# A hybrid encoder layer: rotary rows of q and k gathered into one tile by transfers, turned together and taken back

## The chip, the cores and the metric

The kernel runs on one core of one Trainium2 chip, in one launch. The metric is the device time of an execution in microseconds (us). The kernel before takes 788.81 us (median of three runs, 788.7 to 789.13).

## What is computed

One layer for 512 tokens of width 1024, all in float32. Cut to what matters here:

```python
def rope_partial(t, pos):            # ROT_DIM = 16 of HEAD_DIM = 64, half = 8
    t1, t2, tp = t[..., :half], t[..., half:ROT_DIM], t[..., ROT_DIM:]
    return jnp.concatenate([t1 * cos - t2 * sin, t1 * sin + t2 * cos, tp], axis=-1)

proj = h @ w_in[l]                   # 16 heads of q and 4 of k, v (A); 12 heads of q, k, v (B)
qa, ka, va, qb, kb, vb = jnp.split(proj, SPLITS, axis=-1)
qa, ka, qb, kb = (rope_partial(x, pos) for each, by heads)
o_a = windowed_gqa_sink(qa, ka, va, a_sink[l])       # mixer A: |i - j| <= 128, a sink per head
o_b = dilated_mixture(qb, kb, vb)                    # mixer B: three dilated windows, merged
g_a, g_b = jnp.split(jax.nn.sigmoid(h @ w_gate[l] + b_gate[l]), N_BRANCH, axis=-1)
y = (g_a * (o_a @ w_br_a[l]) + g_b * (o_b @ w_br_b[l])) @ w_out[l]
h = layer_norm(DN_ALPHA * h + y, ln1_g[l], ln1_b[l])
f = (jax.nn.silu(h @ w_ff_gate[l]) * (h @ w_ff_up[l])) @ w_ff_down[l]
h = layer_norm(DN_ALPHA * h + f, ln2_g[l], ln2_b[l])
```

Only the first 16 of each head's 64 features turn; the other 48 pass through.

## The kernel before, in words

**Numbers.** Every float32 operand of a product is split into a high part (rounded to float32r) and a low part (the rest), and a product is three products of parts: high by high, high by low, low by high. Weights arrive as float32 tiles of 128 x 512 (`load`, L335), a copy makes the high part (`copy`, L327 on ACT or L329 on VectorE) and a VectorE subtraction the low one (`split`, L348; in the dense layer `parts` and `tt`, L1091).

**Stages.** The input x, features on partitions, is split into `xh`, `xl` (L424). A unit of 1024 weight columns gives 128 output features by 512 tokens, 24 products of 512 columns (`feat_k`, L448 to L450). Units of q, k, v and the gates run in the order of the string `ORDER`: `q1` is a unit of q for mixer A (two heads), `k1` a unit of its k, `VA` its values, `A0` to `A3` the four head groups of mixer A, `Q01`, `K01` and so on q and k of mixer B, `V0` to `V2` its values, `B0` to `B3` its four heads, `G` a gate unit whose result is stored to DRAM until needed, `g` one that stays. The first units of k, q and v run before the string. Then come the branch products, the output product with the first norm (tokens on partitions, L979 to L981), the dense layer in a Strassen-like form (L1197 to L1199, L1326 to L1328), and the second norm, from which the result is stored.

**q and k.** `dense_q` and `dense_k` put a unit's sum into a PSUM bank. `rotate` (L466) turns all 128 rows, two heads: a product with a cosine table (L468), a shuffle of partitions (L470), a product with a sine table (L472) and a sum (L474). The tables are 128 x 512, with ones and zeros in the rows that don't turn. `q_post` and `k_post` then make the high and low parts of each head (L498, L516).

**Mixer A.** `unit_a` does one group of four heads for 128 tokens: scores (L532, L533), softmax (L654, L658, L614), turns of the probabilities by TensorE (L626), products with the values (L671, L672), and at the end one VectorE sum for each of the four heads (L683) into eight tiles `oaT`. The values of mixer A are turned by TensorE at L565. At most two such units, of A and B together, are under way (`UNITS = 2`).

**The order of the work.** No loop of the source is the order on the engines. `Program` collects every operation with its reads, writes, a priority (the planned PE time at which it is wanted, less a look-ahead: `LOOK` = 130 us for weight loads) and a cost for each engine that may do it. `run` plays these in planned time, gives each engine the most urgent operation that is ready and whose buffers fit, and issues the instructions in that order, so every engine's order is fixed when the program is built. Buffers are counted: 85 tiles of 128 x 512, of them six for arriving weights (`ws`), twelve for split weights (`whl`), 16 for attention, ten for the mixers' results and 41 for the rest (`gen`) as long as attention runs. After the last unit of attention, `free_all` gives the general class 64 and the split weights up to 40 within the whole. In the plan a transfer of SP takes 0.45 us of queue, then 0.65 us and its own cost, and lands 0.9 us later; copies from PSUM (`cp_alts`) may go to ACT or VectorE.

Of the kernel before, what the change touches and what calls it, by code (L numbers as in the profile page):

```python
# [15 lines left out]
P = 128  # L16
S = 512
# [44 lines left out]
N_WS, N_WHL, N_ATT, N_WHL1 = 6, 12, 16, 40  # L62
# [9 lines left out]
VA q1 A0 G q2 q3 G A1 G k1 q4 G q5 A2 G q6 G q7 A3 G2  # L72
Q00 K00 Q01 K01 Q02 K02 V0 V1 V2 B0 B1 g2 Q10 K10 Q11 K11 Q12 K12 B2 B3 g6
# [212 lines left out]
def hybrid_layer(ctx: ExitStack, tc: tile.TileContext, wpack, xT, xtok, sink, bgate,  # L286
# [7 lines left out]
    N_SLOT = 85  # L294
    pr = Program({"slot": N_SLOT, "bank": 8, **BANKS,
                  "ws": N_WS, "whl": N_WHL, "att": N_ATT, "gen": N_SLOT - 10 - N_ATT - N_WS - N_WHL,
                  "unit": UNITS, "st": 4, "x4": 4, "wf": N_WF})
# [53 lines left out]
    LOOK, LOOK_W, LOOK_U, LOOK_T = 130.0, 30.0, 15.0, (-300.0, -118.0, -114.5, -108.0)  # L351

    def half_unit(u, j):
        st, h, l = slot(F32, "ws"), slot(F32R, "whl"), slot(F32R, "whl")
        load(st, wpack[u, :, j * S:(j + 1) * S], prio=-LOOK)
        split(st, h, l, prio=-LOOK, hold=[(l, "room")])
        return h, l
# [29 lines left out]
    def unit(u):  # L387
        return [half_unit(u, 0), half_unit(u, 1)]
# [38 lines left out]
    load(cosT, ropec, abs_prio=-119.5)  # L427
    load(sinT, ropes, abs_prio=-119.4)
# [35 lines left out]
    SHUF = list(range(8, 16)) + list(range(0, 8)) + list(range(16, 32))  # L464

    def rotate(ps):  # L466
        R, Sh = slot(), slot()
        op([(DVE, dve(S))], lambda e: nc.vector.tensor_tensor(R.t, ps.t, cosT.t, op=ALU.mult),  # L468
           reads=[ps, cosT], writes=[R], prio=EV)
        op([(DVE, dve(S, extra=0.03))], lambda e: nc.vector.stream_shuffle(Sh.t, ps.t, SHUF), reads=[ps], writes=[Sh],  # L470
           prio=EV)
        op([(DVE, dve(S))], lambda e: nc.vector.tensor_tensor(Sh.t, Sh.t, sinT.t, op=ALU.mult),  # L472
           reads=[Sh, sinT], writes=[Sh], prio=EV)
        op([(DVE, dve(S))], lambda e: nc.vector.tensor_tensor(R.t, R.t, Sh.t, op=ALU.add),  # L474
           reads=[R, Sh], writes=[R], prio=EV)
        return R

# [8 lines left out]
    def q_post(ps, nt, kv_half):  # L486

        R = rotate(ps)
        out_ = []
        for hh in range(2):  # L490
# [3 lines left out]
            t = slot(F32R)  # L494
            op(cp64(), lambda e, t=t, a=a, hr=hr: copy(
                e, view(t.t[hr:hr + 64], nt, False), view(R.t[a:a + 64], nt, True)),
               reads=[R], writes=[(t, "h"), (t, "room")], prio=EV)
# [3 lines left out]
               reads=[R, (t, "h")], writes=[(t, "l")], prio=EV)  # L501
            out_.append((t, hr))
        return out_

    def k_post(ps, nt):

        R = rotate(ps)
        out_ = []
        for hh in range(2):
            a, c = 64 * hh, 64 - 64 * hh  # L510
            t, kl = slot(F32R), slot(F32R)
            for d, key in ((a, "h"), (c, "d")):
# [122 lines left out]
    oaT = [slot(F32, "res") for _ in range(8)]  # L635
    obT = [slot(F32, "res") for _ in range(2)]

    def unit_a(g, b, qs, kk, vs):
# [47 lines left out]
        lasts.append(op([(DVE, 1.19)], add, reads=[o, t, (U, 0)], writes=[(oaT[2 * g], b), (oaT[2 * g + 1], b)]))  # L686
# [160 lines left out]
    def dense_q(u, nt, kv_half):  # L847
        ps = bank("dense")
        feat_x(ps, unit(u))
        return q_post(ps, nt, kv_half)  # L850

    def dense_k(u, nt):
        ps = bank("dense")
        feat_x(ps, unit(u))
        return k_post(ps, nt)
# [5 lines left out]
    ka = k_post(psk, 4)  # L861
    qa = q_post(psq, 4, (0, 0))
    load(mB, maskb, prio=0)
    env = {"gate": 0, "qs": {}, "ks": {}}

    def step(w):
        if w == "VA":
            env["va"] = turned_values(U_VA, 4, 0, psv)
        elif w[0] == "q":
            i = int(w[1])  # L870
            kv = (i // 2) % 2
            qa.extend(dense_q(U_QA + i, 4, (kv, kv)))
        elif w == "k1":
            ka.extend(dense_k(U_KA + 1, 4))
# [8 lines left out]
        elif w[0] in "QK":  # L883
            pair, g = int(w[1]), int(w[2])
            u = U_QKB + 6 * pair + 2 * g + (w[0] == "K")
            if w[0] == "Q":
                env["qs"][pair, g] = dense_q(u, 4 if g == 0 else 0, (0, 1))
            else:
                env["ks"][pair, g] = dense_k(u, 8 if g == 0 else 0)
# [19 lines left out]
    def split_of(src, toks, prio=0.0):  # L909
        h, l = slot(F32R), slot(F32R)  # L910
        op(cp_alts(S), lambda e: copy(e, h.t, src.t), reads=toks, writes=[h, (l, "room")], prio=prio)
        op([(DVE, dve(S))], lambda e: nc.vector.tensor_tensor(l.t, src.t, f32(h.t), op=ALU.subtract),
# [13 lines left out]
    sa = [split_of(t, [(t, b) for b in range(NR)], -20) for t in oaT]  # L926
# [41 lines left out]
    def tok_major(nk, last, us_of, u0, g, b, finish, fine, alpha=ALPHA):  # L968
# [23 lines left out]
        res = [(k, us_of(k), unit(u0 + k)) for k in range(nk - last, nk)]  # L992
# [113 lines left out]
    TP = {}  # L1106
# [378 lines left out]
```

## Time and profile before

| | us |
|---|---|
| median of 3 runs | 788.81 |
| the profiled execution, its own time | 789.7 |
| its span, first to last instruction | 787.9 |
| PE busy | 776.5 |
| VectorE (DVE) busy | 668.6 |
| ScalarE (ACT) busy | 463.6 |
| GpSimd (POOL) busy | 116.9 |

The granted TensorE clock is 0.998 of 2.4 GHz over the span. PE is TensorE's products, PEld its weight loads, SP the queue that issues most transfers. A row of the trace gives a line of the kernel, an engine, an operation, the tiles it writes and reads (`sl` is any of the 128 x 512 tiles, `ps` a PSUM bank) and what ended the engine's idle time before it. Products overlap, so the length of one is longer than the distance from its start to the next one's.

### The profile page before, as it was taken

What the parts mean: (1) busy time and instruction counts of PE and PEld (TensorE: products, weight loads), DVE (VectorE), ACT (ScalarE), POOL (GpSimd) and SP (SyncE); (2) the same over time, 40 slices, a digit from 0 to 9 for tenths busy, and PEclk for the clock granted to TensorE, in tenths of its full rate; (3) what the DMA queues carried; (4) which work ended last, traced back from release to release, by engine and by line L of the source; (5) the groups of instructions that cost most, each with busy time, mean ns of one, the idle gap of its engine ahead of it and who ended that gap; (6) DMA issues with size and microseconds to landing.
All of it is one profiled execution on the core that took longest, in us unless ns stands there. A gap on an engine that the chain in (4) does not pass through costs nothing.

```text
span 787.9 us, 13456 instructions
## 1 busy us (share of the span) xinstructions
PE 776.5 (99%) x4634; PEld 688.3 (87%) x4634; DVE 668.6 (85%) x1413; ACT 463.6 (59%) x1013; POOL 116.9 (15%) x284
## 2 busy tenths in 40 slices
PE   8999999999999999999999999999999999999995
PEld 5788888888998888888888899999999999999984
DVE  5898999899766999678596999888888889888888
ACT  5655675766755675787251567655655566555710
POOL 0000101000024000610020011133112330123000
PEclk9999999999999999999999999999999999999999
DMA  7533122412131122427563188779876977689102
GB/s 258 210 94 117 58 94 69 141 61 81 44 105 55 51 79 86 173 87 271 169 156 81 41 218 228 185 175 196 225 196 154 233 190 210 179 214 211 53 1 106
DMA packets 61124, 109.42 MB, mean 139 GB/s; under 512 B 7040, under 2 KB 8704, under 8 KB 61056
## 3 DMA queue, kind: packets, MB, share of 16 engines
q1 hardware_dynamic: 49392, 87.53, 33.2%
q0 software_dynamic: 11520, 20.98, 16.1%
q8 instruction: 36, 0.59, 0.3%
q14 instruction: 32, 0.26, 0.1%
q10 hardware_dynamic: 144, 0.07, 0.0%
HBM read 104.35 MB, written 4.19 MB: 138 GB/s over the span
## 4 chain that ended last, share of the span: by engine, by line
PE 92%; DVE 3%; DMA 3%; ACT 1%; SPq 0%; issue 0%; DVEq 0%
PE ps L448 11%; PE ps L449 11%; PE ps L450 11%; PE ps L1199 9%; PE ps L1198 9%; PE ps L1197 9%; PE ps L1326 4%; PE ps L1327 4%; PE ps L1328 4%; PE ps L626 3%; PE ps L979 2%; PE ps L981 2%; PE ps L980 2%; PE ps L533 2%; PE ps L532 2%; DMA sl<-xT 1%
## 5 line engine op out<-in xcount | busy, mean ns | idle before, releaser
L327 ACT ACTIVATE sl<-sl 128x512 fp32r<-128x512 f32 (+3 forms) x420 | 234.0, 587 | 88.4 <-DVE sl L474 34.6
L1091 DVE TENSOR_TENSOR sl<-sl,sl 128x512 fp32r<-128x512 f32 (+3 forms) x308 | 171.9, 603 | 8.7 <-ACT sl L327 7.7
L327 ACT ACTIVATE sl<-ps 128x256 f32<-128x256 f32 (+5 forms) x189 | 83.4, 457 | 103.2 <-PE ps L1199 65.0
L448 PE MATMUL ps<-x,sl 128*128 128x512 f32 x336 | 134.0, 399 | 0.8 <-ACT x L327 0.8
L449 PE MATMUL ps<-x,sl 128*128 128x512 f32 x336 | 131.7, 392 | 0.2 <-DVE x L424 0.2
L450 PE MATMUL ps<-x,sl 128*128 128x512 f32 x336 | 131.2, 391 | 0.0
L1199 PE MATMUL ps<-sl,sl 128*128 128x256 f32 x352 | 99.6, 283 | 0.0
L1198 PE MATMUL ps<-sl,sl 128*128 128x256 f32 x352 | 99.6, 283 | 0.0
L1197 PE MATMUL ps<-sl,sl 128*128 128x256 f32 x352 | 99.5, 283 | 0.0
L348 DVE TENSOR_TENSOR sl<-sl,sl 128x512 fp32r<-128x512 f32 x130 | 87.3, 686 | 14.4 <-ACT sl L327 11.2
L1151 POOL DMA_DIRECT2D sl<-wpack x44 | 40.1, 971 | 256.0 <-DVE sl L1091 96.9
L450 PEld LDWEIGHTS ps<-x,sl 128*128 128x128 f32 x336 | 63.2, 188 | 13.7
L1197 PE MATMUL ps<-x,sl 128*128 128x256 f32 x264 | 74.8, 283 | 0.0
L1199 PE MATMUL ps<-x,sl 128*128 128x256 f32 x264 | 74.7, 283 | 0.0
L1198 PE MATMUL ps<-x,sl 128*128 128x256 f32 x264 | 74.7, 283 | 0.0
L448 PEld LDWEIGHTS ps<-x,sl 128*128 128x128 f32 x336 | 63.3, 188 | 13.0 <-ACT x L327 2.2
L449 PEld LDWEIGHTS ps<-x,sl 128*128 128x128 f32 x336 | 63.4, 189 | 11.6 <-DVE x L424 1.0
L1091 DVE TENSOR_TENSOR sl<-sl,ps 128x512 f32<-128x512 f32 (+1 forms) x78 | 47.2, 610 | 25.0 <-PE ps L1199 15.7
L1197 PEld LDWEIGHTS ps<-sl,sl 128*128 128x128 f32 x352 | 67.5, 192 | 0.8
L1198 PEld LDWEIGHTS ps<-sl,sl 128*128 128x128 f32 x352 | 67.5, 192 | 0.7
L1199 PEld LDWEIGHTS ps<-sl,sl 128*128 128x128 f32 x352 | 67.5, 192 | 0.0
L1197 PEld LDWEIGHTS ps<-x,sl 128*128 128x128 f32 x264 | 50.6, 192 | 0.5
(129 smaller groups left out, 1668.6 us busy)
## 6 DMA issues: line engine op xcount, KB each, us to landing
sl<-wpack SPq DMA_DIRECT2D x243, 256.0 KB, 3.9
sl<-wpack POOLq DMA_DIRECT2D x44, 256.0 KB, 5.3
wf<-wpack SPq DMA_DIRECT2D x36, 256.0 KB, 4.6
wf<-wpack POOLq DMA_DIRECT2D x36, 256.0 KB, 6.3
sl<-xT SPq DMA_DIRECT2D x8, 256.0 KB, 6.3
gz<-sl SPq DMA_DIRECT2D x8, 256.0 KB, 2.1
sl<-gz SPq DMA_DIRECT2D x8, 256.0 KB, 4.9
sl<-xtok SPq DMA_DIRECT2D x8, 256.0 KB, 4.1
```

The lines of the kernel that those rows point to most:

```text
L327: nc.scalar.activation(dst, src, AF.Copy)
L348: op([(DVE, dve(S))], lambda e: nc.vector.tensor_tensor(l.t, src.t, f32(h.t), op=ALU.subtract), reads=[src, h], writes=[l], prio=prio, abs ...
L448: mm(o, a, x0, start=(k == 0), stop=False)
L449: mm(o, a, x1, start=False, stop=False)
L450: mm(o, b, x0, start=False, stop=(k == nk - 1))
L1091: op([(DVE, dve(w))], lambda e: nc.vector.tensor_tensor(dst(), x(), y(), op=o), reads=reads, writes=writes, prio=prio)
L1151: return op([(POOL, 1.0)], lambda e: nc.gpsimd.dma_start(dst.t, wpack[u, :, j * S:(j + 1) * S], accum_op=ALU.add), reads=[dst], writes=[ds ...
L1197: mm(o, wh, bh[k](), start=(first and k == 0), stop=False, skip_group_check=True)
L1198: mm(o, wh, bl[k](), start=False, stop=False, skip_group_check=True)
L1199: mm(o, wl, bh[k](), start=False, stop=(k == 3), skip_group_check=True)
L1326: mm(ps.t, x0, w[0].t, start=(first and m == 0), stop=False, skip_group_check=True)
L1327: mm(ps.t, x0, w[1].t, start=False, stop=False, skip_group_check=True)
```

## The change

The sum of a unit of q or k leaves PSUM by one copy into a tile `raw`. Two transfers on SP take the 16 rows of each head that turn from there into a shared tile, 32 rows for a unit. When `T` stands in `ORDER`, the rows collected so far (two to four units, 64 to 128 rows) are shuffled, multiplied and added as before, and two transfers for each unit take them back into `raw`, from which `q_post` and `k_post` make the parts. There are nine such turns for 22 units. The tables now repeat 16 rows eight times, so they are loaded by eight transfers each, issued by POOL. Mixer A's results lie in four double tiles, and two VectorE sums serve four heads. The four double tiles take the place of eight single ones; after attention they hold two of the dense layer's token forms. The order string moves, and one gate unit changes from stored to staying (seven stored, nine staying). The last weights of the second norm's stage have a look-ahead of 80 us. `dense_q` and `dense_k` become `dense`, which evacuates through `Turn.add`.

```diff
-N_WS, N_WHL, N_ATT, N_WHL1 = 6, 12, 16, 40
+N_WS, N_WHL, N_ATT, N_WHL1, N_TWO = 6, 12, 16, 40, 4
...
 ORDER = """
-VA q1 A0 G q2 q3 G A1 G k1 q4 G q5 A2 G q6 G q7 A3 G2
-Q00 K00 Q01 K01 Q02 K02 V0 V1 V2 B0 B1 g2 Q10 K10 Q11 K11 Q12 K12 B2 B3 g6
+VA q1 T G q2 A0 q3 q4 G k1 T G A1 q5 G q6 q7 T A2 G G A3 G
+Q00 K00 T Q01 K01 T Q02 K02 T V0 V1 V2 B0 B1 g2 Q10 K10 T Q11 K11 T Q12 K12 T B2 B3 g7
 """
...
-    N_SLOT = 85
+    N_SLOT = 85 - 2 * N_TWO
...
+    def two(dt=F32R):
+        return Buf("two", None, lambda: slab.tile([P, 2, S], dt, tag="two", bufs=N_TWO, name=name("tw")))
...
-    load(cosT, ropec, abs_prio=-119.5)
-    load(sinT, ropes, abs_prio=-119.4)
+    for t_, src, ap in ((cosT, ropec, -119.5), (sinT, ropes, -119.4)):
+        for i in range(8):
+            op([(POOL, 1.0)], lambda e, t_=t_, i=i, src=src: nc.gpsimd.dma_start(t_.t[16 * i:16 * i + 16], src[0:16]),
+               writes=[(t_, i)], abs_prio=ap, moves=0.1)
...
-    def rotate(ps):
...
+    SHUF = [*range(8, 16), *range(0, 8), *range(24, 32), *range(16, 24)]
+
+    class Turn:
+        def __init__(self):
+            self.m, self.t = [], slot()
+
+        def add(self, ps, post, *args):
+            raw, n = slot(), len(self.m)
+            op(cp_alts(S, True), lambda e: copy(e, raw.t, ps.t), reads=[ps], writes=[raw], prio=EV)
+            for hh in range(2):
+                op([(SP, 0.1)], lambda e, a=64 * hh, d=32 * n + 16 * hh: nc.sync.dma_start(
+                    self.t.t[d:d + 16], raw.t[a:a + 16]), reads=[raw], writes=[(self.t, n, hh)], prio=EV)
+            heads = [tuple(slot(F32R) for _ in range(1 + (post is k_post))) for _ in range(2)]
+            self.m.append((raw, heads, post, args))
+            return [post.head(h, hh, *args) for hh, h in enumerate(heads)]
+
+        def turn(self):
+            n = len(self.m)
+            t, w = self.t, slot()
+            r = slice(0, 32 * n)
+            toks = [(t, i, hh) for i in range(n) for hh in range(2)]
+            op([(DVE, dve(S, extra=0.03))], lambda e: nc.vector.stream_shuffle(w.t[r], t.t[r], SHUF), reads=toks,
+               writes=[w], prio=EV)
+            op([(DVE, dve(S))], lambda e: nc.vector.tensor_tensor(t.t[r], t.t[r], cosT.t[r], op=ALU.mult),
+               reads=[*toks, *[(cosT, i) for i in range(8)]], writes=[t], prio=EV)
+            op([(DVE, dve(S))], lambda e: nc.vector.tensor_tensor(w.t[r], w.t[r], sinT.t[r], op=ALU.mult),
+               reads=[w, *[(sinT, i) for i in range(8)]], writes=[w], prio=EV)
+            op([(DVE, dve(S))], lambda e: nc.vector.tensor_tensor(t.t[r], t.t[r], w.t[r], op=ALU.add),
+               reads=[t, w], writes=[t], prio=EV)
+            for i, (raw, heads, post, args) in enumerate(self.m):
+                for hh in range(2):
+                    op([(SP, 0.1)], lambda e, raw=raw, a=64 * hh, d=32 * i + 16 * hh: nc.sync.dma_start(
+                        raw.t[a:a + 16], t.t[d:d + 16]), reads=[t, raw], writes=[(raw, hh)], prio=EV)
+                post(raw, heads, *args)
...
-    oaT = [slot(F32, "res") for _ in range(8)]
+    oa2 = [two(F32) for _ in range(4)]
...
         def add(e):
-            for h in range(4):
-                a = 64 * (h % 2)
-                dst = oaT[2 * g + h // 2].t[a:a + 64].rearrange("p (r t i) -> p t r i", r=4, t=4)[:, b]
-                c = slice(h * P, (h + 1) * P)
-                nc.vector.tensor_tensor(dst, o.t[0:64, c].rearrange("p (r i) -> p r i", r=4),
-                                        t.t[0:64, c].rearrange("p (r i) -> p r i", r=4), op=ALU.add)
+            for a in range(2):
+                dst = oa2[g].t[64 * a:64 * a + 64].rearrange("p m (r t i) -> p m r t i", r=4, t=4)[:, :, :, b]
+                x, y = [v[0:64].rearrange("p (m a r i) -> p m a r i", m=2, a=2, r=4)[:, :, a] for v in (o.t, t.t)]
+                nc.vector.tensor_tensor(dst, x, y, op=ALU.add)
...
+    env = {"gate": 0, "qs": {}, "ks": {}, "turn": Turn()}
+    ka = env["turn"].add(psk, k_post, 4)
+    qa = env["turn"].add(psq, q_post, 4, (0, 0))
...
-        res = [(k, us_of(k), unit(u0 + k)) for k in range(nk - last, nk)]
+        res = [(k, us_of(k), unit(u0 + k, LOOK if last < nk else LOOK_E)) for k in range(nk - last, nk)]
```

## Rows read from the trace of the kernel before

**Rows 1.** The page, busy us by engine (share of the span) and instructions.

```profile
PE 776.5 (99%) x4634; PEld 688.3 (87%) x4634; DVE 668.6 (85%) x1413; ACT 463.6 (59%) x1013; POOL 116.9 (15%) x284
```

**Rows 2.** Stages: from:to us, length, busy us by engine, PE clock, DMA share, GB/s.

```profile
core 0: us, PE busy (x) PEld busy (x) DVE busy (x) ACT busy (x) POOL busy (x), PEclk, DMA share, GB/s
0.00:40.00 40.00, 36.93 (x153) 27.52 (x154) 28.80 (x60) 22.70 (x41) 2.00 (x16) 1.00 0.68 230
40.00:220.00 180.00, 180.00 (x947) 154.44 (x947) 165.44 (x398) 120.09 (x274) 12.27 (x44) 1.00 0.25 84
220.00:360.00 140.00, 140.00 (x807) 122.13 (x806) 111.46 (x292) 96.89 (x227) 32.62 (x144) 1.00 0.29 98
360.00:420.00 60.00, 60.00 (x266) 49.72 (x265) 44.64 (x73) 25.40 (x44) 5.35 (x6) 1.00 0.64 187
...
460.00:760.00 300.00, 300.00 (x2152) 284.16 (x2151) 260.66 (x492) 178.71 (x381) 62.88 (x72) 1.00 0.74 184
```

**Rows 3.** Waits of PE: line, waited for, us in total, times, longest us.

```profile
PE ps L448 <- ACT x L327: 0.8, 2, 0.7
PE ps L565 <- ACT sl L327: 0.8, 1, 0.8
PE ps L449 <- DVE x L424: 0.2, 1, 0.2
```

**Rows 4.** PE's timeline at 11 to 14 us: start us, us, what, idle before.

```profile
11.46 0.39 PE L449 MATMUL ps<-x,sl 128*128 128x512 f32 x1
11.69 0.39 PE L450 MATMUL ps<-x,sl 128*128 128x512 f32 x1
12.74 0.51 PE L448 MATMUL ps<-x,sl 128*128 128x512 f32 x1 [0.66 <-ACT x L327]
13.46 0.51 PE L449 MATMUL ps<-x,sl 128*128 128x512 f32 x1 [0.22 <-DVE x L424]
```

**Rows 5.** Groups by line and shape, 0 to 360 us: busy us, mean ns.

```profile
L327 ACT ACTIVATE sl<-ps 128x512 fp32r<-128x512 f32 x48 | 27.0, 596 | 15.6 <-PE ps L626 15.2
...
L683 DVE TENSOR_TENSOR sl<-ps,sl 64x128 f32<-64x128 f32 x64 | 18.0, 282 | 5.8 <-ACT sl L327 5.0
...
L470 DVE STREAM_SHUFFLE sl<-ps 128x512 f32<-128x512 f32 x22 | 16.3, 739 | 0.0
...
L468 DVE TENSOR_TENSOR sl<-ps,sl 128x512 f32<-128x512 f32 x22 | 15.1, 686 | 1.1 <-PE ps L450 0.9
L474 DVE TENSOR_TENSOR sl<-sl,sl 128x512 f32<-128x512 f32 x22 | 15.1, 685 | 0.1
L472 DVE TENSOR_TENSOR sl<-sl,sl 128x512 f32<-128x512 f32 x22 | 15.1, 684 | 0.1
```

**Rows 6.** VectorE's timeline: 22 splits in a row, and a sum of 256 columns.

```profile
457.21 13.39 DVE L1091 TENSOR_TENSOR sl<-sl,sl 128x512 f32<-128x512 f32 x22
...
747.48 0.42 DVE L1091 TENSOR_TENSOR sl<-sl,ps 128x256 f32<-128x256 f32 x1
```

**Rows 7.** SP's timeline: weight loads issued in a row.

```profile
16.80 11.63 SPq L335 DMA_DIRECT2D sl<-wpack  x17
...
44.14 2.77 SPq L335 DMA_DIRECT2D sl<-wpack  x6
```

**Rows 8.** Transfers: size, median us from issue to landing (40 to 330 us; last: whole run).

```profile
sl<-wpack SPq DMA_DIRECT2D x81, 256.0 KB, 3.0
gz<-sl SPq DMA_DIRECT2D x8, 256.0 KB, 2.1
sl<-gz SPq DMA_DIRECT2D x8, 256.0 KB, 4.9
...
out<-sl SPq DMA_DIRECT2D x2, 128.0 KB, 2.0
```

**Rows 9.** POOL's transfers by line: ns min/median/max, first and last start.

```profile
L1151 POOL DMA_DIRECT2D sl<-wpack x44: 862/865/1576, 397.4 to 709.9; - x44
```

**Rows 10.** Two microseconds of the start, columns as in the stages.

```profile
6.00:8.00 2.00, 2.00 (x9) 1.67 (x9) 1.52 (x5) 1.00 (x3) 0.00 (x0) 1.00 0.71 245
```

**Rows 11.** ACT's timeline ahead of the wait at 32 us.

```profile
28.92 3.24 ACT L327 ACTIVATE sl<-sl 64x512 fp32r<-64x512 f32 x5 [1.56 <-DVE sl L474]
```

More of the change, by code (lines that the diff above doesn't have):

```diff
@@ L349, in split, with half_unit @@
            reads=[src, h], writes=[l], prio=prio, abs_prio=abs_prio)
-    LOOK, LOOK_W, LOOK_U, LOOK_T = 130.0, 30.0, 15.0, (-300.0, -118.0, -114.5, -108.0)
-    def half_unit(u, j):
+    LOOK, LOOK_E, LOOK_W, LOOK_U, LOOK_T = 130.0, 80.0, 30.0, 15.0, (-300.0, -118.0, -114.5, -108.0)
+    def half_unit(u, j, look=LOOK):
         st, h, l = slot(F32, "ws"), slot(F32R, "whl"), slot(F32R, "whl")
-        load(st, wpack[u, :, j * S:(j + 1) * S], prio=-LOOK)
-        split(st, h, l, prio=-LOOK, hold=[(l, "room")])
+        load(st, wpack[u, :, j * S:(j + 1) * S], prio=-look)
+        split(st, h, l, prio=-look, hold=[(l, "room")])
         return h, l
@@ L385, in wtok, with unit @@
         return b
-    def unit(u):
-        return [half_unit(u, 0), half_unit(u, 1)]
+    def unit(u, look=LOOK):
+        return [half_unit(u, 0, look), half_unit(u, 1, look)]
     ident = fixed([P, P], "ident")
@@ L484, in view, with q_post @@
         return ap.rearrange("p (t r i) -> p t r i", r=4, t=nt)
-    def q_post(ps, nt, kv_half):
-        R = rotate(ps)
-        out_ = []
+    def q_post(R, heads, nt, kv_half):
         for hh in range(2):
@@ L845, in gate, with dense @@
             away[f] = d
-    def dense_q(u, nt, kv_half):
+    def dense(u, *post):
         ps = bank("dense")
         feat_x(ps, unit(u))
[L850 to L855, printed above, removed]
+        return env["turn"].add(ps, *post)
     psk, psq, psv = bank("dense"), bank("dense"), bank("dense")
@@ L886, in step @@
             if w[0] == "Q":
[L887 removed]
+                env["qs"][pair, g] = dense(u, q_post, 4 if g == 0 else 0, (0, 1))
             else:
[L889 removed]
+                env["ks"][pair, g] = dense(u, k_post, 8 if g == 0 else 0)
         elif w == "V0":
@@ L910, in split_of @@
         h, l = slot(F32R), slot(F32R)
-        op(cp_alts(S), lambda e: copy(e, h.t, src.t), reads=toks, writes=[h, (l, "room")], prio=prio)
-        op([(DVE, dve(S))], lambda e: nc.vector.tensor_tensor(l.t, src.t, f32(h.t), op=ALU.subtract),
+        src = src if callable(src) else lambda b=src: b.t
+        op(cp_alts(S), lambda e: copy(e, h.t, src()), reads=toks, writes=[h, (l, "room")], prio=prio)
+        op([(DVE, dve(S))], lambda e: nc.vector.tensor_tensor(l.t, src(), f32(h.t), op=ALU.subtract),
            reads=[*toks, h], writes=[l], prio=prio)
@@ L925, in hybrid_layer @@
            reads=[gz[f]], writes=[gz[f]], after=exps)
-    sa = [split_of(t, [(t, b) for b in range(NR)], -20) for t in oaT]
+    sa = [split_of(lambda t=t, m=m: t.t[:, m], [(t, b) for b in range(NR)], -20) for t in oa2 for m in range(2)]
     MA = moving(sa)
@@ L1106, in hybrid_layer, with hl_in @@
     TP = {}
+    twos = [N_TWO]
+    def hl_in(st, toks, prio):
+        if twos[0] > 0:
+            twos[0] -= 1
+            t = two()
+            h, l, ht, lt, room = lambda: t.t[:, 0], lambda: t.t[:, 1], (t, "h"), (t, "l"), (t, "room")
+        else:
+            th, tl = slot(F32R), slot(F32R)
+            h, l, ht, lt, room = lambda: th.t, lambda: tl.t, th, tl, (tl, "room")
+        parts((h, ht), (l, lt, room), lambda: st.t, toks, S, prio)
+        return h, l, [ht, lt]
     def token_forms():
```

60 lines of the change are left out of this document (21 added, 39 removed).

## The prediction

> **What bounds the kernel now.** I read the page's sums first, then the stages, then TensorE's own waits, because a change that mostly moves VectorE's work is worth only what TensorE waits for. On the page PE is busy 776.5 of 787.9 us, DVE 668.6 [rows 1]. The table by stages shows that this is no average over unlike stages: from 40 to 360 us, where q, k, both mixers and the gates are made, PE is busy in every microsecond, and so it is from 460 to 760; only the first 40 us (36.93 busy) and the end are short [rows 2]. DVE is busy 92% of 40 to 220 us, so it looks like a second bound, but after the warm-up products PE's waits name ACT for 0.8 us twice and DVE for 0.2 once in the whole run, all before 33 us [rows 3]. A busy PE could still be a slow PE. The timeline answers that: 512-wide products start 0.22 to 0.23 us apart, back to back, although one is shown as 0.39 long [rows 4].
>
> The Trainium skill ("Trainium Kernel Development and Optimization", Performance Expectations) says that matmul busy time is a bad metric for the distance to roofline, and that the share of weight loading is a good one. By that rule the 86% (154.44 of 180) of 40 to 220 us against the 95% (284.16 of 300) of 460 to 760 would be some 9% of 180, an estimated 16 us, that an unburdened VectorE could give back. The trace disagrees: 360 to 420 us, where no attention runs, shows 83% (49.72 of 60) with 266 products of 512 columns in 60 us, the same 0.226 each [rows 2, 4], so the share follows the width of the products and not VectorE's load. The rule stands as a rival below.
>
> So the time is PE's own work, which the change leaves alone (the same products and turns, in another order), plus what PE waits at the start, plus the end.
>
> **Part by part.** *Turning.* Removed: 22 times the four VectorE instructions of `rotate`, 0.686 + 0.739 + 0.684 + 0.685 = 2.79 us each time, 61.5 us [rows 5]. Added: nine turns of the same four, at most 25.1 us (fewer rows, the same 512 columns), and 22 evacuations of 128 x 512, 0.596 us each on ACT, 13.1 us [rows 5]. *Mixer A's sums.* 64 sums of 64 x 128 at 0.282 us, 18.0 us, become 32 of 64 x 256; a sum of 256 columns takes 0.42 us (here on 128 rows), so 13.4 us [rows 5, 6]. Together VectorE loses 36 + 5 = 41 us, ACT gains up to 13. Both lie beside a PE that waits for neither after 33 us: 0 us on the path, whichever engine takes the copies.
>
> *The way there and back.* 88 transfers of 16 rows, 32 KB each, on SP. SP issues one every 0.46 us when the queue is free (six in 2.77) and every 0.68 when it is full (17 in 11.63) [rows 7], so 40 to 60 us of SP's time over some 270 us, and 2.9 MB in all. Behind them in SP's order stand weight loads, which are planned 130 us ahead and have six staging tiles; a load that starts some us late costs 0. No row shows a transfer of SBUF to SBUF of this size. Bounds: 2.0 us (an output of 128 KB that finds the queue empty) and 4.9 us (the eight `gz` loads, 256 KB each, one behind the other), with the weight loads of this stage at 3.0 between; I take 2.1, the `gz` stores, the only SBUF sources in this stage [rows 8]. A turn then delays its first scores by 0.6 (copy) + 0.46 + 2.1 (there) + 2.1 (back) = 5.3 us against today's four instructions, and by 5 x 0.46 = 2.3 us more for the last of three members: 5.3 to 7.6 us; at 4.9 a way, 10.9 to 13.2. The cover is in ORDER: behind the first turn stand a gate and q2, each 24 products at 0.227, 10.9 us; before the last two units of mixer B stand seven gates (38 us) instead of six. Price 0 as long as the order on PE holds that cover where it is needed and landings stay under 4.9; without it the 5.3 to 7.6 us would stand on PE.
>
> VectorE's turn now waits for a landing, with weight splits and softmax steps of VectorE queued behind it. If each of nine turns holds VectorE up by 1 us, that is 9 us out of the 41 set free: 0 on the path.
>
> *Rope tables.* Two SP loads of 256 KB behind the loads of x become 16 loads of 32 KB from POOL, which nothing holds back. POOL's transfers take 0.865 us each to issue [rows 9], so they run from about 0.5 to 14.4 us, beside the first tiles of x and weights. POOL's next work, the copies for mixer A, starts after 18 us, so POOL's own queue costs 0. PE waits for x at 12.74 and 13.46 us [rows 4], so this delay is on the path. Below: 0, as DMA is only 71% busy from 6 to 8 us [rows 10]. Above: the 13 loads issued by 12 us, 0.43 MB at that stage's 245 GB/s, 1.7 us. I take +0.5, nearer to the idle share, since 29% of 12 us leaves 3.5 us of room. SP's later loads come two issues, some 1.4 us, sooner; they are not late for PE: 0.
>
> *The wait at 32 us.* PE waits 0.8 us at L565 for a value tile that ACT copies after five copies for k's heads, which had waited for L474 [rows 3, 11]. With the turn put off behind q1, ACT evacuates the values first: -0.8. Bounds 0 (the next tile is late instead) and -0.8.
>
> *Slots.* 77 tiles and four double ones instead of 85. While attention runs, the general class has 41 either way. Afterwards the doubles serve only two token forms, so weights for the dense layer are split ahead into some two tiles fewer: one pair of copy and subtraction, about 0.6 + 0.7 us, moves behind 457 us, where VectorE runs 13.39 us without a gap [rows 6] and PE waits for nothing: 0, at most +1.3. *One stored gate fewer, and the later look-ahead of the last weights:* DMA is far from full there and the last chain is VectorE's norm, unchanged: 0 within 0.4.
>
> Sum against the profiled execution: 789.7 - 0.8 + 0.5 = 789.4 us. That execution is 0.9 above the median of the three runs, 788.81 (span 787.9, 1.8 around it), so **788.5 us**. A measurement of this kernel can tell about 0.2%, 1.6 us, from no change.
>
> **The rivals.** *The start gives more (faster).* If VectorE and ACT, with less to do, also shorten the waits for x (0.66 and 0.22 us) and the tables cost nothing, the gain is 0.8 + 0.88 = 1.7 us: 787.1 us. For it: ACT and DVE are the releasers named. Against it: ACT itself waits there for DMA, which gets more to carry. 0.18.
>
> *Landings come late at the first scores (slower).* The order on PE is fixed in the program by a plan that gives a small transfer 0.45 + 0.65 + 0.1 + 0.9 = 2.1 us. If landings take 3.0 us like this stage's weight loads on the same queue [rows 8], scores stand in PE's order 2 x 0.9 = 1.8 us too early; behind a burst, at 4.9, 5.6 us. It decides where a turn's scores are the next thing PE was planned to do: the first unit of mixer A and the third of mixer B (in between, two units at a time hold attention back, not q and k). Over both places that is 3.6 us, 792.1 us, and at most 11.2, 799.7 us. For it: the queue is shared, and a load in front must drain first. Against it: the `gz` stores land in 2.1 us on the same queue. 0.17.
>
> *PE is slow under VectorE's load (the page's rule above).* 788.5 - 16 = 772.5 us by the mechanism that weight loading could run denser; the pace in [rows 4] speaks against it. 0.02.
>
> *Tables and slots at their upper ends:* 788.81 - 0.8 + 1.7 + 1.3 = 791.0 us, slower. 0.06.
>
> **How the numbers follow.** The forecast, within 0.2%, gets 0.57. Faster: 0.18 + 0.02 = 0.20; slower: 0.17 + 0.06 = 0.23. The range goes from 786.7 (the start's gain and 0.4 for the end) to 791.3 (tables and slots at their ends, and 0.3); it leaves out the late landings and the denser weight loading, 0.19.
>
> **What would show it.** Right: PE still busy in every microsecond from 40 to 360 us, no wait of PE on ACT at the value turns, DVE's sum 35 to 45 us lower with the same span, small transfers landing near 2.1 us. The tables' price shows in when the first products of the third and fourth slice of x start (11.7 to 13.5 us now). Wrong: waits of PE at the score products or at the turns of probabilities behind a turn, small landings of 3 us and more, or a gap of PE between the last unit of mixer B and the branch products.

## The result and the profile after

The kernel after takes 792.82 us (median of 4 runs, 791.61 to 793.4) beside 788.75 us for the kernel before on the same chip: a ratio of 1.0048, with a 95% interval of 1.0036 to 1.006. It is slower by some 4 us, outside the range that was predicted. The profiled execution took 793.4 us, its span is 791.6.

The page's sums of the kernel after, which answer to [rows 1]:

```profile
PE 778.7 (98%) x4634; PEld 689.1 (87%) x4634; DVE 642.0 (81%) x1333; ACT 469.1 (59%) x1018; POOL 126.0 (16%) x300
```

VectorE has 26.6 us less to do, as the change means it to, and the span is 3.7 us longer. The stages say where; these rows answer to [rows 2], with the stage of 360 to 420 us cut finer below it:

```profile
0.00:40.00 40.00, 38.36 (x156) 27.79 (x157) 22.64 (x48) 18.87 (x35) 10.04 (x28) 1.00 0.74 230
40.00:220.00 180.00, 180.00 (x965) 155.18 (x964) 155.81 (x360) 131.78 (x293) 14.37 (x52) 1.00 0.30 95
220.00:360.00 140.00, 140.00 (x794) 122.07 (x793) 104.67 (x269) 97.30 (x224) 31.60 (x140) 1.00 0.33 106
360.00:420.00 60.00, 57.90 (x247) 47.15 (x246) 41.41 (x67) 21.49 (x36) 4.05 (x5) 0.97 0.51 159
...
406.00:408.00 2.00, 0.36 (x2) 0.32 (x3) 2.00 (x4) 1.41 (x3) 0.00 (x0) 1.00 0.00 0
408.00:410.00 2.00, 2.00 (x8) 1.58 (x7) 2.00 (x5) 1.12 (x3) 0.00 (x0) 0.68 0.03 8
410.00:412.00 2.00, 2.00 (x6) 1.56 (x5) 2.00 (x4) 1.79 (x4) 0.00 (x0) 0.50 0.00 0
412.00:414.00 2.00, 2.00 (x10) 1.63 (x9) 2.00 (x4) 0.00 (x0) 0.00 (x0) 0.97 0.00 0
```

PE is fuller at the start (38.36 us of 40, where a second profile of the kernel before, below, has 37.53), and the whole stretch in which q, k and attention are made has no gap, in spite of 88 small transfers. The loss stands in one place, where the output product begins: PE is idle for most of 406 to 408 us, and from 408 to 412 us the granted clock falls to 0.68 and then 0.50, which is the lower level, 1.2 GHz. In 360 to 420 us PE starts 247 products where it started 266.

PE's waits [rows 3] name the place. The wait at 32 us on the value tile is gone, and a new one stands ahead of the others:

```profile
PE ps L1001 <- DVE sl L969: 2.0, 1, 2.0
...
PE ps L453 <- ACT x L330: 0.2, 1, 0.2
PE ps L454 <- DVE x L427: 0.2, 1, 0.2
```

PE's timeline around it; the last column is the idle time before an instruction and what ended it:

```profile
405.21 0.40 PE L1003 MATMUL ps<-sl,sl 128*128 128x512 f32 x1
407.64 0.50 PE L1001 MATMUL ps<-sl,sl 128*128 128x512 f32 x1 [2.03 <-DVE sl L969]
...
408.67 0.58 PE L1002 MATMUL ps<-sl,sl 128*128 128x512 f32 x1
409.05 0.63 PE L1003 MATMUL ps<-sl,sl 128*128 128x512 f32 x1
...
411.61 0.63 PE L1003 MATMUL ps<-sl,sl 128*128 128x512 f32 x1
412.04 0.44 PE L1001 MATMUL ps<-sl,sl 128*128 128x512 f32 x1
```

L1001 to L1003 are the three products of parts of the output product (L979 to L981 before). It collects eight PSUM banks, four blocks of tokens by two halves of the width. The bank of the product at 407.64, the eighth, was last used by the branch products, and VectorE's L969, which multiplies it with its gate, has to read it first. The loss can be counted in the rows: from 405.21 to 407.64 one step of 0.23 us took 2.43, 2.2 too many; from 408.67 to 412.04 eight steps took 3.37 us where eight at 0.227 take 1.81, 1.6 too many. Some 0.5 us more goes in steps of 0.28 to 0.46 around them.

Why VectorE is late is one row further up. VectorE's timeline of the kernel after:

```profile
395.08 0.69 DVE L969 TENSOR_TENSOR sl<-sl,ps 128x512 f32<-128x512 f32 x1
395.74 0.69 DVE L934 TENSOR_TENSOR sl<-sl,sl 128x512 fp32r<-128x512 f32 x1
399.68 0.69 DVE L934 TENSOR_TENSOR sl<-sl,sl 128x512 fp32r<-128x512 f32 x1 [3.25 <-PE ps L454]
...
406.90 0.68 DVE L969 TENSOR_TENSOR sl<-sl,ps 128x512 f32<-128x512 f32 x1
```

The same stretch before has no gap:

```profile
397.49 1.27 DVE L947 TENSOR_TENSOR sl<-sl,ps 128x512 f32<-128x512 f32 x2
398.69 0.68 DVE L912 TENSOR_TENSOR sl<-sl,sl 128x512 fp32r<-128x512 f32 x1
399.29 1.28 DVE L949 TENSOR_TENSOR sl<-sl,sl 128x512 f32<-128x512 f32 x2
```

L934 (L912 before) writes the low part of a mixed token block, `sm`. Its operands come from ACT and VectorE, yet it waits for PE's L454, a branch product: it seems to need the tile that this product reads. So **a free tile** is missing. The kernel's own plan (`Program.used`, counted as the program is built) says so too: when the first block of `sm` is split, all 77 tiles are taken, 30 of them in the general class, 38 by split weights and nine by arriving ones, with no double tile in use; the kernel before has 82 of its 85 taken there. The general class is not at its own limit (56); the whole is. VectorE's order is fixed, and the gate multiplications (L969) that empty the PSUM banks stand behind the split. From 399.68 to 406.90 it runs without a gap and does not catch up.

**Theory S (slots).** The four double tiles take eight tiles out of the 85 that all classes share. At 395 us the 77 that are left are full and the doubles stand empty, so a split waits for PE; that costs 2 us of idle PE and then the lower clock. **Rivals:** the turning itself (its transfers, the new order) makes VectorE late there; the later load of the token weights does; or the clock falls for another reason than PE's idleness.

### The profile page after: what moved, and what is told of

Its sections match the earlier page's. It is cut to its first block, busy times and chain, and to the rows that moved or that the text cites. A ratio compares the mean times of both kernels' runs of the same rounds, so it can differ in the third digit from the quotient of the medians.

```text
span 791.6 us, 13596 instructions
## 1 busy us (share of the span) xinstructions
PE 778.7 (98%) x4634; PEld 689.1 (87%) x4634; DVE 642.0 (81%) x1333; ACT 469.1 (59%) x1018; POOL 126.0 (16%) x300
## 4 chain that ended last, share of the span: by engine, by line
PE 95%; DVE 4%; DMA 1%; issue 0%; SPq 0%; DVEq 0%
PE ps L454 12%; PE ps L453 12%; PE ps L455 12%; PE ps L1231 9%; PE ps L1230 9%; PE ps L1229 9%; PE ps L1358 4%; PE ps L1359 4%; PE ps L1360 4%; PE ps L651 3%; PE ps L1001 2%; PE ps L1003 2%; PE ps L558 2%; PE ps L1002 2%; PE ps L557 2%; PE ps L697 1%
## 5 line engine op out<-in xcount | busy, mean ns | idle before, releaser
L330 ACT ACTIVATE sl<-sl 128x512 fp32r<-128x512 f32 (+3 forms) x424 | 236.7, 588 | 74.3 <-PE ps L454 14.4
L1113 DVE TENSOR_TENSOR sl<-sl,sl 128x512 fp32r<-128x512 f32 (+3 forms) x304 | 169.5, 603 | 8.4 <-ACT sl L330 7.5
L330 ACT ACTIVATE sl<-ps 128x256 f32<-128x256 f32 (+4 forms) x196 | 88.2, 466 | 119.1 <-PE ps L1231 67.8
L454 PE MATMUL ps<-x,sl 128*128 128x512 f32 x336 | 131.9, 393 | 0.2 <-DVE x L427 0.2
L351 DVE TENSOR_TENSOR sl<-sl,sl 128x512 fp32r<-128x512 f32 x130 | 86.7, 686 | 18.8 <-ACT sl L330 17.0
L455 PEld LDWEIGHTS ps<-x,sl 128*128 128x128 f32 x336 | 63.1, 188 | 14.2 <-DVE sl L379 0.6
L454 PEld LDWEIGHTS ps<-x,sl 128*128 128x128 f32 x336 | 63.3, 188 | 12.7 <-DVE x L427 2.1
L453 PEld LDWEIGHTS ps<-x,sl 128*128 128x128 f32 x336 | 63.3, 188 | 12.1 <-ACT x L330 1.2
L1229 PEld LDWEIGHTS ps<-x,sl 128*128 128x128 f32 x264 | 50.6, 192 | 0.5
L1230 PEld LDWEIGHTS ps<-x,sl 128*128 128x128 f32 x264 | 50.6, 192 | 0.5
L1231 PEld LDWEIGHTS ps<-x,sl 128*128 128x128 f32 x264 | 50.6, 192 | 0.0
L1231 PE MATMUL ps<-tw,sl 128*128 128x256 f32 x176 | 49.8, 283 | 0.0
L1230 PE MATMUL ps<-tw,sl 128*128 128x256 f32 x176 | 49.8, 283 | 0.0
L1231 PE MATMUL ps<-sl,sl 128*128 128x256 f32 x176 | 49.8, 283 | 0.0
L1229 PE MATMUL ps<-tw,sl 128*128 128x256 f32 x176 | 49.8, 283 | 0.0
```

The costliest lines, as they stand in the source:

```text
L330: nc.scalar.activation(dst, src, AF.Copy)
L453: mm(o, a, x0, start=(k == 0), stop=False)
L454: mm(o, a, x1, start=False, stop=False)
L455: mm(o, b, x0, start=False, stop=(k == nk - 1))
L1113: op([(DVE, dve(w))], lambda e: nc.vector.tensor_tensor(dst(), x(), y(), op=o), reads=reads, writes=writes, prio=prio)
L1229: mm(o, wh, bh[k](), start=(first and k == 0), stop=False, skip_group_check=True)
```

## The experiments

Every ratio below is to the kernel before on the same chip.

**turn_alone.** The turning, the new order, the tables and the 80 us look-ahead, without the doubles:

```diff
-    N_SLOT = 85 - 2 * N_TWO
+    N_SLOT = 85
...
-    oa2 = [two(F32) for _ in range(4)]
+    oaT = [slot(F32, "res") for _ in range(8)]
...
-    twos = [N_TWO]
+    twos = [0]
```

> The changed kernel's turning, order string, table loads and 80 us look-ahead, but the eight single result tiles, the four sums a unit and 85 tiles of the kernel before; no double tiles. Theory S (tiles): the changed kernel's wait of TensorE at 405 us (2.0 us on VectorE, then products at half the clock for some 4 us) comes from the tiles given up, so it is gone here: TensorE busy 60.00 of 60 us from 360 to 420, no idle of VectorE over 1.5 us between 391 and 404 us, time 787.0 to 788.2 us (the start's gain of 1.2 to 1.4 us is kept). Theory T (turning): the wait comes with the transfers, the moved order or the ninth staying gate: it is still there, time 791 to 793 us.

Measured: 789.06 us (788.78 to 790.04), ratio 1.0005 [0.9996, 1.0014]. PE has no wait behind 360 us, and the stage is full again:

```profile
360.00:420.00 60.00, 60.00 (x266) 49.67 (x266) 40.95 (x67) 22.06 (x37) 5.25 (x6) 1.00 0.61 176
```

The turning does not make the stall. But the gain expected of the start did not come in the medians; turn_tables_sp below finds it.

**doubles_alone.** The other half: the kernel before with the four doubles, two sums at a time and the shorter look-ahead, and the old `rotate`.

```diff
-    N_SLOT = 85
+    N_SLOT = 85 - 2 * N_TWO
...
-    LOOK, LOOK_W, LOOK_U, LOOK_T = 130.0, 30.0, 15.0, (-300.0, -118.0, -114.5, -108.0)
+    LOOK, LOOK_E, LOOK_W, LOOK_U, LOOK_T = 130.0, 80.0, 30.0, 15.0, (-300.0, -118.0, -114.5, -108.0)
...
-    oaT = [slot(F32, "res") for _ in range(8)]
+    oa2 = [two(F32) for _ in range(4)]
```

> The kernel before with its own rotation and order string, but the four double tiles for mixer A's results, the two sums a unit, 77 tiles and the 80 us look-ahead of the changed kernel. Theory S: the wait of TensorE at the start of the output product appears here too, 2.0 us and the clock's loss, 360 to 420 us busy 56 to 58.5 of 60, time 792.5 to 794.5 us (worse than the changed kernel, since the start's gain is missing). Theory T: no such wait, 788.0 to 789.5 us.

Measured: 794.11 us (792.24 to 794.23), ratio 1.006 [1.0047, 1.0072]. The wait stands there without any turning, as long as after:

```profile
PE ps L981 <- DVE sl L949: 2.0, 1, 2.0
```

By the medians the doubles with their look-ahead cost 794.11 - 788.82 = 5.3 us here, more than the 4.0 found below; the five times spread (two near 792.3, three near 794.2), and the rest of the difference was not settled.

**after_whl32.** Split weights may hold eight tiles fewer of the 77, so eight more are left to the others.

```diff
-N_WS, N_WHL, N_ATT, N_WHL1, N_TWO = 6, 12, 16, 40, 4
+N_WS, N_WHL, N_ATT, N_WHL1, N_TWO = 6, 12, 16, 32, 4
```

> The changed kernel with one number changed: at most 32 instead of 40 tiles for split weights after attention, so that some tiles stay free while the mixed rows are split. Theory S: VectorE's idle before its second split of the mixed rows (3.25 us at 396 to 400) is under 1 us, TensorE doesn't wait at 405 us, time 787.8 to 789.0 us (the tail's 0.7 us stays). Theory T: as the changed kernel, 791.6 to 793.4 us; if fewer split weights hurt the dense layer, more.

Measured: 790.35 us (789.81 to 790.68), ratio 1.0019 [1.0011, 1.0028]. The stall is gone; the stretch in which it stood:

```profile
404.00:408.00 4.00, 4.00 (x19) 3.30 (x18) 4.00 (x8) 2.75 (x6) 1.73 (x2) 1.00 0.84 179
```

The median is 1.35 us above the range that was expected. In the profiles PE's last product starts 0.9 us later than in after_sm_doubles below (778.60 beside 777.66 us) and the end behind it is 0.5 us longer. That the split weights miss their eight tiles is likely, but not shown.

**after_look130.** The look-ahead of the last weights back at 130 us.

```diff
-    LOOK, LOOK_E, LOOK_W, LOOK_U, LOOK_T = 130.0, 80.0, 30.0, 15.0, (-300.0, -118.0, -114.5, -108.0)
+    LOOK, LOOK_E, LOOK_W, LOOK_U, LOOK_T = 130.0, 130.0, 30.0, 15.0, (-300.0, -118.0, -114.5, -108.0)
```

> The changed kernel with the last weights' look-ahead at 130 us again instead of 80. Two questions. If the 80 us are what puts the last dense-layer products 0.7 us later in TensorE's order than before, the tail from TensorE's last product to the end falls from 9.0 to 8.3 us and the time by 0.7. If 130 us with 77 tiles takes tiles that the last dense-layer products need, TensorE waits near 750 us, 1 to 3 us, and the time is 793 to 796 us. I lean to the second.

Measured: 794.25 us (793.15 to 794.37), ratio 1.0066 [1.0052, 1.008]. The stall at 405 us is unchanged, and PE waits for VectorE in the dense layer's last part too:

```profile
759.58 0.50 PE L1358 MATMUL ps<-sl,sl 128*128 128x512 f32 x1 [0.21 <-DVE sl L1113]
760.78 0.50 PE L1359 MATMUL ps<-sl,sl 128*128 128x512 f32 x1 [0.70 <-DVE sl L1113]
```

VectorE is late there because it makes eight splits of the last weights (L351) in a row, ahead of the sums and splits that PE needs; first after_look130, then the kernel after, which makes at most three at a time:

```profile
752.84 4.90 DVE L351 TENSOR_TENSOR sl<-sl,sl 128x512 fp32r<-128x512 f32 x8
```

```profile
757.64 1.89 DVE L351 TENSOR_TENSOR sl<-sl,sl 128x512 fp32r<-128x512 f32 x3
```

The time expected came, but not for the reason expected: in the plan at most 62 of the 77 tiles are taken there. The kernel before, with 130 us and 85 tiles, has no such wait; why was not settled. So with the doubles the shorter look-ahead helps, by 1.4 us of the medians, with ranges that just overlap.

**after_sm_doubles.** The cure by theory S: the doubles' empty room is used at the very point where tiles are short.

```diff
+class Half:
+    def __init__(self, whole, i):
+        self.whole, self.i = whole, i
+
+    @property
+    def t(self):
+        return self.whole.t[:, self.i]
...
-    def split_of(src, toks, prio=0.0):
-        h, l = slot(F32R), slot(F32R)
+    def split_of(src, toks, prio=0.0, pair=None):
+        h, l = (Half(pair, 0), Half(pair, 1)) if pair else (slot(F32R), slot(F32R))
...
-        sm.append(split_of(gz[f], [gz[f]], EV))
+        sm.append(split_of(gz[f], [gz[f]], EV, two() if f < 3 else None))
```

> The kernel after, with one change: the high and low parts of three of the four mixed token blocks (sm) stand in three of the four double tiles, which lie idle at that point, so six tiles of the general class stay free ahead of the output product. Nothing is computed otherwise. Theory S (the doubles take eight tiles out of the common class; ahead of the output product VectorE's split of the mixed rows waits for a tile, so the eighth PSUM bank is emptied late, PE stands still for 2 us and then runs at half clock): VectorE's wait before L934 and PE's wait at the first product of the eighth bank are gone, the clock stays above 0.95 in 404 to 416 us, and the time is 788.5 to 790.0 us, the end's loss of some 0.7 us staying. Rival (the stall comes from the later loads of the token weights, not from tiles): the wait stays and the time is 792 to 793.5 us.

Measured: 788.83 us (788.64 to 789.28), ratio 1.0003 [0.9994, 1.0012]. VectorE's wait of 3.25 us is 0.50 now, PE's is gone, and the clock stays up:

```profile
400.07 1.29 DVE L944 TENSOR_TENSOR sl<-sl,sl 128x512 fp32r<-128x512 f32 x2 [0.50 <-PE ps L464]
```

```profile
360.00:420.00 60.00, 60.00 (x266) 49.73 (x265) 40.97 (x67) 21.09 (x35) 5.20 (x6) 1.00 0.61 179
```

The same instructions with six tiles elsewhere are 792.82 - 788.83 = **4.0 us** faster than the kernel after (the kernel before took 788.75 and 788.8 beside the two). That is the price of the missing tiles in the kernel after, with the clock's part in it, and as much as the whole loss against the kernel before.

**after_fill.** Is the lower clock PE's idleness, or something else that happens there? VectorE is left as late as it is, and PE gets something to do while it waits.

```diff
+                for _ in range(9 if (nk, k, t, j) == (KD, 0, NR - 1, 1) else 0):
+                    mm(acc[t, 0].t, warm[:, :P], warm, start=False, stop=False, skip_group_check=True)
...
```

> The kernel after, with nine extra 512-wide products of a zero tile added into the first accumulator bank just before the product that waits (they add zeros), so that PE works through the 2 us in which it stood idle. VectorE is as late as before, so the wait itself is not cured. If the half clock behind the stall is PE's own idleness, the clock stays above 0.95 in 406 to 414 us and the time is 790.3 to 791.3 us, some 2 us below the kernel after (the stall of 2 us stays as filled time). If the half clock has another cause (the load of several engines at once), the products behind it are still 0.43 us apart and the time stays at 792.3 to 793.5 us.

Measured: 791.57 us (791.36 to 791.94), ratio 1.0037 [1.0025, 1.005]. The product is as late as in the kernel after (407.83 us beside 407.64), VectorE's wait is the same 3.25 us, but what follows runs at the upper level, 2.4 GHz:

```profile
405.63 2.12 PE L1002 MATMUL ps<-warm 128*128 128x512 bf16 x9
407.83 0.50 PE L1003 MATMUL ps<-sl,sl 128*128 128x512 f32 x1
```

```profile
408.00:410.00 2.00, 2.00 (x9) 1.63 (x10) 2.00 (x4) 0.93 (x2) 0.00 (x0) 1.00 0.00 0
410.00:412.00 2.00, 2.00 (x10) 1.69 (x9) 2.00 (x5) 1.93 (x4) 0.00 (x0) 1.00 0.00 0
```

The clock, then, follows PE's own idle time. The rows of PE's last product give the price; first the kernel after, then after_fill:

```profile
782.17 0.39 PE L1003 MATMUL ps<-sl,sl 128*128 128x512 f32 x1
```

```profile
780.74 0.39 PE L1005 MATMUL ps<-sl,sl 128*128 128x512 f32 x1
```

From the product that was late to this one it is 374.5 us after and 372.9 us with the filling: 1.6 us, as counted above. The medians give 792.82 - 791.57 = 1.25 us, a little less than expected. The four times after lie apart (791.61, 792.29, 793.35 and 793.4), the five of after_fill together; whether the clock falls in the shorter executions too is not shown. It falls in each profiled execution that has this stall: in doubles_alone and after_look130 the lowest 2 us show 0.50 as well.

**before_again.** Is the first profile of before typical?

> The kernel before, unchanged, profiled once more. If the profile of before is typical, the span is 787.5 to 788.3 us, PE's first wait on the value tile (0.8 us at L565) and the first output product at 401.7 us come again within 0.2 us, and the 1.1 us by which turn_alone reached that product sooner is real. If it was one execution's accident, the first output product lies 0.5 us or more elsewhere.

Measured: 789.01 us (788.19 to 789.53), ratio 1.0002 [0.9993, 1.0012]; span 786.9, where the first profile had 787.9. The wait on the value tile comes again, somewhat shorter:

```profile
PE ps L565 <- ACT sl L327: 0.6, 1, 0.6
```

The first output product starts at 400.71 us, not at 401.71; the first profile of before, then this one:

```profile
401.71 0.39 PE L979 MATMUL ps<-sl,sl 128*128 128x512 f32 x1
```

```profile
400.71 0.39 PE L979 MATMUL ps<-sl,sl 128*128 128x512 f32 x1
```

The second option holds: the start of this kernel moves by about 1 us from one execution to the next, and turn_alone's 400.62 us is no lead. From here on medians decide what the start is worth.

**turn_tables_sp, turn_tables_again.** turn_alone with the tables in their old place on SP.

```diff
-    for t_, src, ap in ((cosT, ropec, -119.5), (sinT, ropes, -119.4)):
-        for i in range(8):
-            op([(POOL, 1.0)], lambda e, t_=t_, i=i, src=src: nc.gpsimd.dma_start(t_.t[16 * i:16 * i + 16], src[0:16]),
-               writes=[(t_, i)], abs_prio=ap, moves=0.1)
+    load(cosT, ropec, abs_prio=-119.5)
+    load(sinT, ropes, abs_prio=-119.4)
```

> The kernel of turn_alone, with the two rope tables loaded by SP as two transfers of 256 KB in their old place, instead of sixteen of 32 KB from POOL (the tables repeat the 16 rows eight times). It prices the tables alone. By the prediction's term (+0.5 us, bounds 0 and 1.7): 788.3 to 788.8 us against 789.06 for turn_alone, and the first output product about 0.5 us sooner than its 400.62 us. If the sixteen small transfers cost nothing, 789.0 to 789.3; if the two large loads hold back x and the weights behind them on SP's queue, 789.5 to 790.5 us.

Measured: 787.49 us (787.41 to 790.64, ten of eleven under 788), ratio 0.9989 [0.998, 0.9998]. It is 1.57 us under turn_alone (the kernel before took 788.82 and 788.8 beside the two). ACT's copies of the second and third part of x show what the tables did; first turn_alone, then turn_tables_sp:

```profile
6.19 0.63 ACT L330 ACTIVATE x<-sl 128x512 fp32r<-128x512 f32 x1 [0.95 <-DMA sl<-xT]
8.75 0.63 ACT L330 ACTIVATE x<-sl 128x512 fp32r<-128x512 f32 x1 [0.96 <-DMA sl<-xT]
```

```profile
5.64 0.63 ACT L330 ACTIVATE x<-sl 128x512 fp32r<-128x512 f32 x1 [0.63 <-DMA sl<-xT]
7.92 0.63 ACT L330 ACTIVATE x<-sl 128x512 fp32r<-128x512 f32 x1 [1.01 <-DMA sl<-xT]
```

x comes 0.55 and 0.83 us sooner when the tables stand behind it. The other profiles of kernels with the turns agree: 5.55 and 5.68, 7.85 and 8.25 us with the tables on SP, 6.25 to 7.69 and 8.96 to 9.37 with them on POOL. Since the interval ends near 1, the kernel was measured once more:

> The kernel of turn_tables_sp once more, unchanged, to settle whether it beats the kernel before: its first interval, 0.998 to 0.9998, ends at 1. If its gain is real, the ratio is 0.998 to 0.9995 again (787.2 to 788.4 us) and the first output product lies near 399.4 us; if the first comparison was lucky, the ratio is 0.9995 to 1.0005 (788.4 to 789.1).

787.81 us (787.29 to 788.5), ratio 0.9989 [0.998, 0.9998] again. The gain is 0.9 to 1.3 us, about the least that such comparisons can tell; both favour this version over the kernel before and over the kernel after.

**turn_tables_pool2.** The tables from POOL at the start again, but as two transfers of 256 KB.

> The kernel of turn_tables_sp with its two tables as two transfers of 256 KB issued by POOL at the start, so the same bytes as in turn_alone at the same time, in 2 transfers instead of 16. If the bytes ahead of x cost the time (0.52 MB at some 250 GB/s are 2 us of the queues), it is 788.7 to 789.3 us, as turn_alone. If the number of transfers costs it, it is 787.3 to 787.8, as turn_tables_sp.

Measured: 789.05 us (788.65 to 789.61), ratio 1.0005 [0.9996, 1.0014]; turn_alone, with sixteen, had 789.06. Two transfers cost what sixteen did, so it is the 0.5 MB ahead of x that cost, not the number of transfers. The Trainium skill ("DMA: Bandwidth & Descriptors", Rules for kernel authors) advises to join many small transfers into a large one, since under 64 KB one pays mostly overhead; here, where they run ahead of other loads, joining them changed nothing that can be measured.

**before_tables_pool.** The tables' move alone, in the kernel before.

> The kernel before with the two rope tables loaded as sixteen transfers of 32 KB from POOL at the start, and nothing else changed. If the tables cost 1.2 to 1.6 us by holding back the loads of x, the time is 790.0 to 790.4 us, ACT's second and third part of x start 0.3 to 0.8 us later, and the wait on the value tile at L565 stays. If the tables cost only together with the new order of the turns, it is 788.6 to 789.1. The prediction's term would give 789.3.

Measured: 789.24 us (788.59 to 789.81), ratio 1.0006 [0.9997, 1.0015]: 0.5 us, not told from none, and less than the 1.2 to 1.6 us. The expectation that the wait at L565 stays was wrong: PE's waits of this execution hold none on the value tile (L403 is a warm-up product),

```profile
PE ps L403 <- DVE eps L437: 1.2, 1, 1.2
PE ps L451 <- DVE x L424: 0.2, 1, 0.2
```

ACT's second and third part of x start at 6.43 and 9.50 us, later than in both profiles of before (5.97 and 5.74, 8.20 and 9.04). This fits a PE that is later by the tables and meets the value tile ready: part of the tables' price would hide in a wait that the kernel before has anyway (0.8 and 0.6 us in its two profiles), and with the turns in their new order, which removes that wait, nothing would be left to hide it. It rests on one trace, and the start moves by 1 us between executions, so it is argued and not shown.

**smd_tables_sp.** Both cures together, on the kernel after.

> The kernel of after_sm_doubles with the two rope tables loaded by SP in their old place, as in turn_tables_sp: the kernel after with both of the suspected faults taken out. If the two act apart from each other, the time is 788.83 less the 1.24 us (first output product) to 1.57 us (medians) that the tables were worth in turn_tables_sp: 787.3 to 787.6 us, level with turn_tables_sp, which has no doubles. If the doubles cost something of their own beyond the tiles (the end of the kernel, where the last chunk stands one step earlier before the end), it is 787.9 to 788.5. If they gain beyond the tiles, it is under 787.2.

Measured: 788.04 us (787.64 to 788.8), ratio 0.9995 [0.9986, 1.0004]. It is 0.8 us under after_sm_doubles, so the tables count here too, and 0.2 to 0.55 us above the two measurements without doubles: no gain of the doubles is left to see. Whether their small loss is real (PE's last product starts 9.3 us before the end of the span here, 8.8 in turn_tables_sp) can't be told.

## Why the prediction was wrong

**The step that failed is the one on slots.** It said that, with fewer tiles, weights for the dense layer are split ahead into some two tiles fewer, and one copy and subtraction move behind 457 us: 0, at most +1.3. The runs showed 4.0 us (after against after_sm_doubles), at another place: 50 us earlier, where a split finds no free tile while the doubles are idle, and the one who waits is not a weight split far ahead of its use but a split that is due, on the engine that also empties PSUM. The step let the weights that are split ahead give way; in the plan they hold 38 of the 77 tiles, and the split that is due finds none. It went by 457 us, where PE waits for nothing [rows 2], and not by the point where the tiles are fullest. And it had no term for what an idle PE does to the clock, 1.25 us of the 4.0 by the medians and 1.6 by the rows.

The step on the look-ahead, 0 within 0.4, looked at DMA and not at VectorE's order: with 130 us and the doubles VectorE makes the last weights' splits ahead of due work, and PE waits 0.9 us near 760 us. The end, which it held unchanged, is longer: PE's last product starts 9.4 us before the end of the span after and 8.6 before, 0.8 us more where 0.4 was the bound; 9.0 of it stay in after_look130, so the look-ahead makes about half of that, and the other half is open.

**Rope tables.** +0.5, between 0 and 1.7, was the right mechanism and too small: 1.25 and 1.57 us (turn_alone less the two measurements of turn_tables), 0.8 us with the doubles, 0.5 in the kernel before. The argument for the low end, a queue 29% idle in [rows 10], was weak: the question was what goes ahead of x, and the DMA's share in 4 to 8 us rises from 0.74 to 0.97 with the tables in it; the kernel before, then the kernel after:

```profile
4.00:8.00 4.00, 3.82 (x12) 2.27 (x11) 3.07 (x10) 2.06 (x6) 0.00 (x0) 1.00 0.74 239
```

```profile
4.00:8.00 4.00, 3.75 (x12) 1.97 (x10) 2.36 (x8) 2.16 (x6) 3.36 (x8) 1.00 0.97 263
```

The duration it went by, 0.865 us for each of POOL's transfers [rows 9], was that of 128 rows; those of 16 rows take 0.5, so all sixteen are out by 10 us, not 14.4:

```profile
1.28 4.02 POOL L432 DMA_DIRECT2D sl<-ropec  x8 [0.83 <-POOLq L1505]
```

**The wait at 32 us.** -0.8 was right: the wait is in no kernel with the turns, and without tables and doubles these gain 0.9 to 1.3 us. The first rival, a start that gives 1.7 us, lies above that.

**The turning and the way there and back** were priced at 0, and that held: PE is busy in every microsecond from 40 to 360 us in the kernel after (turn_alone has one wait of 0.3 us there), and turn_tables_sp is not slower. The small transfers land in 1.9 us, where 2.1 was taken from the `gz` stores [rows 8]:

```profile
sl<-sl SPq DMA_DIRECT2D x88, 32.0 KB, 1.9
```

The Trainium skill ("DMA: Bandwidth & Descriptors", Anatomy of one DMA) gives a transfer a fixed part of about 2.0 us and 436 GB/s; that is for POOL's path and makes an estimated 2.1 us for 32 KB. SP's 1.9 us, on another path, come near it. The rival of late landings, which named 792.1 us and more, comes near the time and is wrong in its mechanism: VectorE and ACT wait for a turn's transfers, there (L493) and back (L332, L330), and PE for none.

```profile
DVE sl L493 <- DMA sl<-sl: 3.3, 3, 1.7
...
DVE sl L332 <- DMA sl<-sl: 2.6, 4, 1.1
```

```profile
ACT sl L330 <- DMA sl<-sl: 11.6, 5, 6.4
```

**VectorE's sum** fell by 26.6 us, not by 35 to 45. Of the 22 evacuations, all put on ACT in the sum, 12 went to VectorE:

```profile
L332 DVE COPY sl<-ps 128x512 f32<-128x512 f32 x12 | 8.2, 689 | 4.5 <-PE ps L455 4.4
```

The scalings of the probabilities (L616 before, L641 after), which either engine may do, are most of the rest: 43 of those with 256 and 384 columns stand on VectorE after and 27 before, 5.3 us more. The sums of mixer A took 13.3 us, as priced (13.4). It made no difference to the time, as the prediction said: PE does not wait for VectorE there. The rival from the page on the share of weight loading is out: VectorE has less to do, and PEld goes from 154.44 to 155.18 in 40 to 220 us.

**The sum by the runs:** 788.7 - 0.9 to 1.3 (turns in their new order) + 0.8 to 1.6 (tables) + 4.0 (tiles) gives 792.2 to 793.4 us; 792.8 was measured. The terms come from the same runs, so this shows that nothing large is left over, not that each term is right.

## What to carry to other kernels

When a change takes tiles out of a common pool, count what is alive at the pool's fullest point (a program that plans its own order can print it), and ask which engine waits there and what stands behind that instruction in its order; an average over stages does not show it, and a double tile is idle room for whoever is short beside it. A gap of PE costs more than its length, because the products behind it may run at the lower clock, so the first thing to look for in a stage that got slower is a wait followed by a drop of the granted clock. Small transfers at the start are paid by what they delay: put what is needed late behind what is needed first.

## What the hardware showed that was not expected

An idle time of 2.03 us ahead of one product, with 0.36 us of products in 406 to 408 us, was followed by a clock of 0.50, and the drop came not at once: the products are slow from 408.7 to 412.0 us, when PE was busy again. With the same 2 us filled by nine products of a zero tile, the clock stayed at 1.00. The Trainium skill ("TensorE: Matmul & The Clock Gate", Loop structure matters more than you think) holds a copy out of PSUM harmless as long as the next products follow at once, and a long wait for DMA harmful. The runs fit this with an addition: here the operation that empties PSUM was the harm, as it came late for the bank that the next product needed.

The price of the same early transfers differed between kernels: 0.5 us, not told from none, in one that waits a little later anyway, up to 1.6 us in one that doesn't. And the start of one unchanged kernel moved by 1 us between two executions, as much as the change's own gain there.
